# Three intermediates of a recurrent layer kept in PSUM between VectorE's steps

## The chip, the cores and the metric

The kernel runs on one core of a Trainium2 chip. The metric is device time in microseconds (us), as the median of several runs. Engines are named as in the profile: PE (TensorE, matmuls), PEld (its weight loads), DVE (VectorE), ACT (ScalarE), POOL (GpSimd), and SP, which here only issues DMAs. SBUF is the large on-chip memory; PSUM is the small one that matmuls write, used here as eight banks of 128 partitions by 512 fp32 values. PE, DVE and ACT work on PSUM here; POOL and DMAs work on SBUF only.

## The reference

Two layers of a decoder, 512 tokens, width 1024, all in fp32. Layer 0 is an RWKV-7 time mixing: token-shifted mixes of the normalised input go through four projections (r, k, v and a gate g), and then a recurrence runs over time for each of 16 heads, with a 64x64 state:

```python
def step(state, inp):
    r_t, w_t, k_t, v_t, kk_t, a_t = inp
    s_kk = jnp.einsum('bhij,bhj->bhi', state, kk_t)
    state = (state * w_t[:, :, None, :]
             - s_kk[..., None] * (kk_t * a_t)[:, :, None, :]
             + v_t[..., None] * k_t[:, :, None, :])
    return state, jnp.einsum('bhij,bhj->bhi', state, r_t)
```

Its result y is normalised per head, a bonus term is added, and it is multiplied by silu(g) and projected by `w_out`. Each layer ends with a gated per-layer embedding ("ple"). Layer 1 is a causal differential attention on keys and values projected from layer 0's result. Only layer 0 is touched here.

## The kernel before

**Dense products.** Every projection is made of 128x512 blocks. For accuracy an fp32 operand is split into a high and a low part in fp32r, and one block product is three matmuls (lines 285, 286 and 287: high by high, high by low, low by high). I call such a triple a block; 800 of them make up most of PE's work. Weights arrive by DMA (`RAW`), ACT or DVE rounds the high part (line 270) and POOL or DVE subtracts it to get the low part (line 318).

**The recurrence, in chunks.** Time is cut into 8 chunks of 64 tokens, and the 16 heads into two groups of 8 (g = 0 and 1). `gram` multiplies keys by queries inside a chunk pair (line 984) and DVE masks the result into SBUF tiles `G` (line 993). `inverse(n)` inverts the small triangular matrices, for four batches of (group, half of time): it gathers 32x32 blocks of `G` into a tile `na` (line 270, on ACT or DVE by a planner's choice), loads a unit matrix `eye32` by DMA and copies it by ACT into a PSUM bank `xs` (line 1030), transposes `na` on DVE (line 1042), does 31 steps of substitution on DVE (lines 1051 and 1054), transposes back (1060, 1075) and finishes with two rounds of 32x32 matmuls on PE (1087, 1101) and small copies back into `G` (270 and 1115, eight of these on ACT). `operands` transposes the keys of a chunk (1149, 1152). `recur(g)` then does one chunk after the other: products with `G` (1188), the product with the state `S_` (1201), two pairs of copies from PSUM (270) with a product between them, the update product `pS` (1229), and the new state on DVE: the sum with `pS` (line 1241) and the decay (line 1244). `finish(cq, g)` normalises y (1284 to 1293), transposes it on PE (1304), adds a bias and multiplies by the gate on DVE (line 1310), and splits the result `zF` into high (270) and low (1318) for the output projection.

**What sets the order.** All this is written as Python generators. A planner (`Streams`) runs while the program is built: each `yield` names an engine (or two to choose from), an estimated cost, a buffer taken or freed, or an event; the planner keeps a clock for each engine and always takes the step that can start first, by its own estimates. A `+` after an engine's name means that the step also takes a port that the planner shares between DVE and POOL. The instructions stand on each engine's queue in the order in which the planner took them, and each queue runs in order. So a change of a cost, an engine or a buffer in one place can move instructions of the whole stage. Buffers are counted: 43 slots `R` and 9 slots `H` in SBUF, and eight PSUM banks, four for dense blocks (`pd`) and four for everything else (`pw`). Dense blocks of the projections fill PE while the recurrence waits for other engines.

## Time and profile before

| | |
|---|---|
| median of 3 runs | 792.98 us (791.94 to 794.04) |
| the profiled execution | 797.09 us, span 795.3 us |
| PE busy | 756.1 us (95%) |
| DVE busy | 589.8 us (74%) |
| ACT busy | 454.5 us (57%) |
| POOL busy | 201.9 us (25%) |
| from 80 to 407 us (recurrent stage) | 327.0 us, PE busy 309.45 us, DVE 280.96 us |
| from 407 us to the end | 388.3 us, PE busy 379.04 us |

Busy time is the time in which an engine has an instruction in work. The granted clock of PE (PEclk) is 1.00 nearly everywhere and lower in a few stretches. What counts for the time is where PE has nothing to do or runs at the lower clock: all other engines have room on average, but each may be the one that PE waits for at a given place. Spans on POOL are rough.

### The profile page before, as it was taken

To read this page: it belongs to the slowest core of one execution; us is meant where nothing else is said; L and a number is where in the kernel's file an instruction comes from. 1 tells how busy PE (TensorE), PEld (TensorE's weight loads), DVE (VectorE), ACT (ScalarE), POOL (GpSimd) and SP (SyncE) were. 2 spreads that over 40 slices of the span, in tenths; PEclk is the share of its full clock that TensorE was granted. 3 is DMA by queue.
4 is the path that set the end of the run, shared out by engine and by line. 5 is a ranking of instruction groups with operands and counts; after the bars stand their busy time and mean duration, and the time that the engine had idled before them with its cause. 6 is when DMAs were issued, how large, how long until landed. Compare 5 with 4: busy or idle time off the path is not lost.

```text
span 795.3 us, 13941 instructions
## 1 busy us (share of the span) xinstructions
PE 756.1 (95%) x5016; PEld 605.1 (76%) x5016; DVE 589.8 (74%) x1360; ACT 454.5 (57%) x1078; POOL 201.9 (25%) x221
## 2 busy tenths in 40 slices
PE   6899999998999899999989999999999999999996
PEld 3576578875777677777778888887888888888884
DVE  2989999976798898998676685446874768835844
ACT  3779745688875446664444564333764566743431
POOL 2416615521451425666010010000000001100000
PEclk9999999998999899999999999999999999999998
DMA  8585669843684687463446444488943523314602
GB/s 325 197 285 196 245 225 290 298 147 105 209 286 171 217 301 258 145 228 105 133 166 247 133 146 135 172 309 226 312 158 92 159 53 121 117 43 159 259 6 106
DMA packets 66677, 148.79 MB, mean 187 GB/s; under 512 B 6576, under 2 KB 27312, under 8 KB 66608
## 3 DMA queue, kind: packets, MB, share of 16 engines
q1 hardware_dynamic: 43824, 112.25, 41.9%
q10 hardware_dynamic: 22784, 35.66, 13.1%
q8 instruction: 39, 0.64, 0.3%
q14 instruction: 30, 0.25, 0.1%
HBM read 110.13 MB, written 37.75 MB: 186 GB/s over the span
## 4 chain that ended last, share of the span: by engine, by line
PE 70%; DVE 8%; ACT 8%; DMA 8%; issue 2%; POOL 2%; SPq 1%; ACTq 0%; POOLq 0%; DVEq 0%
PE p L285 18%; PE p L287 18%; PE p L286 18%; PE p L1788 2%; PE p L984 2%; PE p L1188 2%; ACT R L270 1%; PE p L1753 1%; PE p L1752 1%; PE p L1201 1%; DMA R<-bD 1%; PE p L1779 1%; DMA RAW<-in_ple_w 1%; PE p L1410 1%; DMA R<-mD 1%
## 5 line engine op out<-in xcount | busy, mean ns | idle before, releaser
L285 PE MATMUL p<-R,R 128*128 128x512 f32 x800 | 326.4, 408 | 3.2 <-DVE R L270 1.7
L286 PE MATMUL p<-R,R 128*128 128x512 f32 x800 | 314.1, 393 | 3.8 <-DVE R L525 3.6
L287 PE MATMUL p<-R,R 128*128 128x512 f32 x800 | 314.4, 393 | 0.0
L285 PEld LDWEIGHTS p<-R,R 128*128 128x128 f32 x800 | 151.3, 189 | 37.1 <-DVE R L270 1.9
L287 PEld LDWEIGHTS p<-R,R 128*128 128x128 f32 x800 | 151.0, 189 | 33.2 <-DVE R L1318 0.4
L286 PEld LDWEIGHTS p<-R,R 128*128 128x128 f32 x800 | 151.5, 189 | 32.4 <-DVE R L525 4.9
L318 POOL TENSOR_TENSOR R<-RAW,R 128x512 fp32r<-128x512 f32 x59 | 78.6, 1339 | 163.3 <-ACT R L270 89.1
L270 ACT CAST R<-RAW 128x512 fp32r<-128x512 f32 x110 | 66.1, 619 | 26.7 <-DMA RAW<-in_w_g 10.0
L318 DVE TENSOR_TENSOR R<-RAW,R 128x512 fp32r<-128x512 f32 x81 | 56.8, 715 | 11.0 <-ACT R L270 10.2
L324 DVE SCALAR_TENSOR_TENSOR R<-RAW,vec,R 128x512 fp32r<-128x512 f32 x64 | 46.6, 748 | 13.9 <-ACT R L322 13.7
L322 ACT ACTIVATE R<-RAW,vec 128x512 fp32r<-128x512 f32 x64 | 44.6, 720 | 17.0 <-DMA RAW<-in_b_w_in 9.1
L1397 POOL TENSOR_TENSOR hr<-hm,half 128x1 f32<-128x1 f32 x16 | 10.4, 648 | 147.2 <-DVE hm L1395 147.2
L1757 DVE CUSTOM_DVE_ANT_0 p<-p,cmask 128x128 f32<-128x128 f32 (+3 forms) x64 | 30.3, 509 | 17.4 <-PE p L1753 17.3
L1764 ACT ACTIVATE H<-p,mx 128x128 f32<-128x128 f32 (+3 forms) x64 | 33.3, 526 | 15.7 <-DVE mx L1761 14.1
L281 POOL TENSOR_TENSOR orr<-orm,half 128x4 f32<-128x4 f32 x8 | 8.4, 1055 | 123.3 <-DVE orm L279 93.3
L1054 DVE TENSOR_TENSOR p<-p,H 128x126 f32<-128x126 f32 (+22 forms) x124 | 32.6, 263 | 4.3
L1051 DVE TENSOR_TENSOR H<-p,R 128x126 f32<-128x126 f32 (+22 forms) x124 | 30.5, 246 | 1.1
L1534 DVE SCALAR_TENSOR_TENSOR R<-H,R 128x512 f32<-128x512 f32 x16 | 11.1, 691 | 24.5 <-ACT H L1527 23.1
L1527 ACT ACTIVATE H<-p 128x512 f32<-128x512 f32 x16 | 9.5, 596 | 31.6 <-PE p L287 31.6
L521 DVE SCALAR_TENSOR_TENSOR p<-R,vec,p 128x511 f32<-128x511 f32 x32 | 23.5, 747 | 5.4 <-ACT p L519 5.3
L519 ACT ACTIVATE p<-R,omm 128x512 f32<-128x512 f32 x32 | 22.0, 695 | 5.0 <-DVE R L525 3.7
L1788 PEld LDWEIGHTS p<-R,H 128*128 128x128 f32 x160 | 22.1, 191 | 2.8 <-ACT H L1805 0.5
(227 smaller groups left out, 1249.4 us busy)
## 6 DMA issues: line engine op xcount, KB each, us to landing
R<-mD SPq DMA_DIRECT2D x40, 512.0 KB, 5.3
mD<-R ACTq DMA_DIRECT2D x32, 512.0 KB, 4.3
RAW<-in_ple_gate SPq DMA_DIRECT2D x16, 512.0 KB, 3.7
RAW<-in_kv_w SPq DMA_DIRECT2D x16, 512.0 KB, 3.9
RAW<-in_b_w_in SPq DMA_DIRECT2D x16, 512.0 KB, 3.9
R<-bD ACTq DMA_DIRECT2D x24, 256.0 KB, 5.2
R<-in_x SPq DMA_DIRECT2D x8, 512.0 KB, 6.8
RAW<-in_w_r SPq DMA_DIRECT2D x8, 512.0 KB, 4.0
```

What stands on the lines that cost most here:

```text
L270: (nc.scalar.copy if sc.eng == "ACT" else ENG[sc.eng].tensor_copy)(dst, src)
L285: nc.tensor.matmul(ps, ah, bh, start=first, stop=False)
L286: nc.tensor.matmul(ps, ah, bl, start=False, stop=False)
L287: nc.tensor.matmul(ps, al, bh, start=False, stop=last)
L318: ENG[sc.eng].tensor_sub(lo, f, hi.bitcast(F32))
L322: nc.scalar.activation(hi, f, AF.Copy, scale=g)
L324: nc.vector.scalar_tensor_tensor(lo, f, g, hi.bitcast(F32), ALU.mult, ALU.subtract)
L1051: ve.tensor_mul(tmp[:, 0:m, 0:w], bc(xs[:, s_ : s_ + 1, 0:w], [P, m, w]), bc(nb[:, s_ + 1 : 32, s_ : s_ + 1], [P, m, w]))
L1054: ve.tensor_add(xs[:, s_ + 1 : 32, 0:w], xs[:, s_ + 1 : 32, 0:w], tmp[:, 0:m, 0:w])
L1757: nc.vector.tensor_tensor_reduce(scs[m][:, 0:n], scs[m][:, 0:n], cmask[:, S - n : S], 1.0, -3.0e38, ALU.add, ALU.max, mx[:, m : m + 1])
L1764: nc.scalar.activation(E[m][:, 0:n], scs[m][:, 0:n], AF.Exp, bias=mx[:, m : m + 1], scale=0.125, accum_out=sm[:, m : m + 1])
L1788: nc.tensor.matmul(po[:, x * P : (x + 1) * P], aT[:, kb * P : (kb + 1) * P], vT[hg, kb // 2][:, kb % 2, x * P : (x + 1) * P], start=(kb == 0),
```

## The change

Three intermediates, all of layer 0's recurrent stage, go from SBUF tiles to PSUM banks. In `inverse`, the gathered tile `na` is a PSUM bank, taken before the gathering; the unit matrix stays in its SBUF slot until the gathering is done, and ACT's copy of it into `xs` now stands behind the gathering; `xs` takes its bank only then. One `H` slot fewer is taken. In `recur`, the sum of state and `pS` is written into `pS`'s bank instead of into the state, and the decay reads it from there. In `finish`, the gated result is written over its own PSUM input, which is held until both halves of the split have read it; the high part is always made by ACT and the low part always by DVE. The planner's marks and costs for these steps change with them (`DVE+!` to `DVE!`, the transpose's 2.0 to 1.14).

```diff
-        yield "take", "H", 3
-        na, xs, tmp = HT([P, 16, 32]), HT([P, 32, 16]), HT([P, 31, 16])
+        yield "take", "H", 2
+        eye, tmp = HT([P, 32, 16]), HT([P, 31, 16])
         yield "DMA!", 0.4
-        nc.sync.dma_start(xs, I["eye32"])
-        if eng == "DVE":
-            yield "take", "pw", 1
-            eye, xs = xs, bank("pw").rearrange("p (s c) -> p s c", c=16)
-            yield "ACT!", 0.52
-            nc.scalar.copy(xs, eye)
-            yield "free", "H", 1
+        nc.sync.dma_start(eye, I["eye32"])
+        yield "take", "pw", 1
+        na = bank("pw").rearrange("p (h t) -> p h t", t=32)
         for u in range(2):
             yield "wait", ("gram", 2 * cp + u, g)
             for hh in range(2):
                 for q, r in enumerate(quads):
-                    yield "ACT/DVE+!", (0.2, 0.2)
+                    yield "ACT/DVE!", (0.2, 0.2)
                     copy(four(na[r, 8 * u + 4 * hh : 8 * u + 4 * hh + 4]), lower(q, u, hh)[:, :, :, 32 * (q % 2) : 32 * (q % 2) + 32])

+        yield "take", "pw", 1
+        xs = bank("pw").rearrange("p (s c) -> p s c", c=16)
+        yield "ACT!", 0.52
+        nc.scalar.copy(xs, eye)
+        yield "free", "H", 1
         yield "take", "R", 1
         nb = R([P, 32, 32])
-        yield "DVE", 2.0
+        yield "DVE", 1.14
         nc.vector.transpose(nb, bc(na.rearrange("p h t -> p t h").unsqueeze(2), [P, 32, 2, 16]))
-        yield "free", "H", 1
+        yield "free", "pw", 1
...
                     if c_ > 0:
                         yield "DVE!", 0.42
-                        nc.vector.tensor_add(sv, sv, qv)
-                        qv = sv
-                    yield "DVE+!", 0.42
+                        nc.vector.tensor_add(qv, qv, sv)
+                    yield "DVE!", 0.42
                     nc.vector.tensor_mul(sv, qv, bc(pcall[hs, c_, 4 * g : 4 * g + 4].unsqueeze(2), [HN, 4, HN]))
...
         for x in range(4):
             xs = slice(x * P, (x + 1) * P)
-            nc.vector.scalar_tensor_tensor(w[:, xs], pt[:, xs], vcol(V_LB, 4 * g + x), gt[:, xs], ALU.add, ALU.mult)
-        yield "free", "pw", 1
+            nc.vector.scalar_tensor_tensor(pt[:, xs], pt[:, xs], vcol(V_LB, 4 * g + x), gt[:, xs], ALU.add, ALU.mult)
...
-        yield "ACT/DVE+", (0.52, 0.34)
-        copy(hi, w)
-        yield "Pool+/DVE+", (1.23, 0.6)
-        ENG[sc.eng].tensor_sub(lo, w, hi.bitcast(F32))
+        yield "ACT", 0.48
+        nc.scalar.copy(hi, pt)
+        yield "DVE", 0.6
+        nc.vector.tensor_sub(lo, pt, hi.bitcast(F32))
+        yield "free", "pw", 1
```

Lines behind the first hunk are moved by one: 1042, 1060, 1087, 1101, 1115, 1152, 1188, 1201, 1229 and 1241 are now 1043, 1061, 1088, 1102, 1116, 1153, 1189, 1202, 1230 and 1242; the copy of the unit matrix goes from 1030 to 1038. From line 1244 on the numbers are the same up to 1310; the split's two lines are now 1315 and 1317.

The planner's order moves with the change, from the gathering of the first inverse on to the end of layer 0's recurrence; in the rest of the program PE's blocks stand in the same order. Three places are shown. Names are a tile's pool (`p` for a PSUM bank, `R` and `H` for SBUF slots) with a number.

The first is ACT's queue at the gathering of the fourth batch; line 1501 empties the banks of the embedding's products. Before:

```order
L1501 COPY H_2970<-p_2935 128x512
L1501 COPY H_2983<-p_2969 128x512
L1030 COPY p_3010<-H_2994 128x512
L270 COPY H_2993<-R_2877 32x128 x3
L270 COPY H_2993<-R_2878 32x128 x3
L1501 COPY H_3005<-p_2982 128x512
L1501 COPY H_3042<-p_3004 128x512
```

And now:

```order
L1501 COPY H_2974<-p_2949 128x512
L270 CAST R_2995<-RAW_2669 128x512
L1501 COPY H_3012<-p_2973 128x512
L1501 COPY H_3027<-p_3011 128x512
L1501 COPY H_3056<-p_3026 128x512
L270 CAST R_3057<-RAW_2846 128x512
L270 COPY p_2979<-R_2961 32x128 x3
L270 COPY p_2979<-R_2962 32x128 x3
L1038 COPY p_3098<-H_2965 128x512
```

The copy of the unit matrix, which needs a DMA, stood ahead of the last two copies of line 1501 and of the gathering; it now stands behind all of them.

The second is ACT's queue behind the second inverse, from its last small copy (1115, now 1116) to the copy (270, out of a `p` bank into `H`) on which the recurrence's next product waits. Before:

```order
L1115 COPY R_1206<-p_1987 32x2x2x32
L1115 COPY R_1206<-p_1988 32x2x2x32
L787 ACTIVATE p_1939<-H_1862 128x512
L270 COPY H_2087<-p_1992 64x2x128
L789 ACTIVATE R_1460<-H_1862 128x4x128
```

And now:

```order
L1116 COPY R_1217<-p_1991 32x2x2x32
L1116 COPY R_1217<-p_1992 32x2x2x32
L872 COPY H_2060<-p_1491 128x512
L872 COPY H_2086<-p_1499 128x512
L523 CAST R_1997<-p_1998 128x512
L519 ACTIVATE p_2008<-R_116,omm_97 128x512
L270 COPY H_2106<-p_2089 64x2x128 x2
```

One ACT instruction stood between them, and half of the copy; now four stand there and the whole copy. Ahead of these rows, from the two copies behind line 1087's matmuls (now 1088) on, ACT's queue holds in the new order four copies of line 1153, one of 872, two of 866, one of 519, nine of 270 and the eight of 1116. On PE, between line 1088's matmuls and the product that waits, now stand four transposes, three blocks and the matmuls of 1102, 1189, 1202 and 824, and a fourth block whose bank the first copy of line 872 shown above empties.

The third is PE's queue at the end of the recurrence: the transposes of the last y (line 1304) and the first block that reads what `finish` makes of it (`R_4621` before, `R_4612` now). Before:

```order
L285 MATMUL p_4363<-R_4282,R_4554 128x512
L286 MATMUL p_4363<-R_4282,R_4554 128x512
L287 MATMUL p_4363<-R_4282,R_4554 128x512
L1304 MATMUL p_4610<-ident_89,R_4101 128x128 x4
L285 MATMUL p_4461<-R_4222,R_4621 128x512
```

And now:

```order
L1304 MATMUL p_4597<-ident_89,R_4082 128x128 x4
L285 MATMUL p_4449<-R_4298,R_4511 128x512
L286 MATMUL p_4449<-R_4298,R_4511 128x512
L287 MATMUL p_4449<-R_4298,R_4511 128x512
L285 MATMUL p_4449<-R_4306,R_4511 128x512
L286 MATMUL p_4449<-R_4306,R_4511 128x512
L287 MATMUL p_4449<-R_4306,R_4511 128x512
L285 MATMUL p_4449<-R_4363,R_4511 128x512
L286 MATMUL p_4449<-R_4363,R_4511 128x512
L287 MATMUL p_4449<-R_4363,R_4511 128x512
L285 MATMUL p_4506<-R_4272,R_4612 128x512
```

No block stood between them, and three do now; counted from the recurrence's last product (line 1188, now 1189), 11 blocks stood ahead of that reading block and 16 do now. On DVE, between the transposes of lines 1042 and 1075 of the third batch, the queue holds one instruction less of each of the lines 684, 993, 1069 and 270, all moved behind that stretch or to ACT. The last six products with the state (1201) stood 11, 11, 8, 7 and 5 blocks apart on PE, and now stand 6, 7, 8, 6 and 5 blocks apart.

More of the change, by code (lines that the diff above doesn't have):

```diff
@@ L1060, in inverse @@
         nc.vector.transpose(xr, bc(xs.unsqueeze(3), [P, 32, 16, 2]))
-        yield ("free", "pw", 1) if eng == "DVE" else ("free", "H", 1)
+        yield "free", "pw", 1
         yield "take", "H", 3
@@ L1314, in finish @@
         hi, lo = (zF[cq, g][:, n].rearrange("p a b -> p (a b)") for n in range(2))
-        yield "ACT/DVE+", (0.52, 0.34)
-        copy(hi, w)
-        yield "Pool+/DVE+", (1.23, 0.6)
-        ENG[sc.eng].tensor_sub(lo, w, hi.bitcast(F32))
+        yield "ACT", 0.48
+        nc.scalar.copy(hi, pt)
+        yield "DVE", 0.6
+        nc.vector.tensor_sub(lo, pt, hi.bitcast(F32))
+        yield "free", "pw", 1
         yield "free", "R", 1
```

## The prediction

> **What bounds the kernel now.** I read the page's busy times first, then a table by stretch, then what ended PE's idle time.
>
> ```profile
> PE 756.1 (95%) x5016; PEld 605.1 (76%) x5016; DVE 589.8 (74%) x1360; ACT 454.5 (57%) x1078; POOL 201.9 (25%) x221
> PE   6899999998999899999989999999999999999996
> PEclk9999999998999899999999999999999999999998
> ```
>
> PE is busy for 95% of the span, and the digits fall below 9 only in a few slices; in two of them PEclk falls too. PE is the bound, so only its idle time and its slow clock can be won. The next rows give, for each stretch, its length, busy time (and count) of PE, PEld, DVE, ACT, POOL, then the granted clock, the share of the DMA engines and GB/s.
>
> ```profile
> 187.10:193.80 6.70, 5.31 (x29) 3.91 (x31) 5.39 (x9) 6.44 (x17) 1.38 (x1) 0.53 0.04 7
> 265.60:272.40 6.80, 6.37 (x27) 5.28 (x28) 5.06 (x13) 5.11 (x13) 3.76 (x3) 0.53 0.46 155
> 250.50:292.85 42.35, 37.62 (x186) 30.08 (x185) 37.59 (x118) 18.12 (x38) 15.04 (x12) 0.92 0.70 249
> 480.00:520.00 40.00, 40.00 (x180) 33.09 (x179) 20.64 (x31) 14.58 (x25) 0.95 (x1) 1.00 0.51 167
> 80.00:407.00 327.00, 309.45 (x2886) 241.69 (x2886) 280.96 (x663) 202.87 (x497) 135.41 (x145) 0.98 0.62 211
> 407.00:795.30 388.30, 379.04 (x1882) 316.88 (x1881) 248.17 (x597) 193.89 (x479) 34.88 (x40) 0.99 0.47 154
> ```
>
> The change touches only the stage from 80 to 407 us. There PE idles 327.0 - 309.45 = 17.6 us, and two stretches of 6.7 and 6.8 us run at a clock of 0.53, which costs a busy PE up to 6.8 x 0.47 = 3.2 us each. So the most that any change here could win is about 24 us; DVE, though busy for 281 of 327 us, is worth only what PE waits for it. The 480 to 520 row gives the price of a block at full clock: 40 us / 180 matmuls x 3 = 0.67 us. The next rows are PE's idle times in this stage that bear on the change: start, length, instruction, and in brackets the idle time before it and what ended it.
>
> ```profile
> 185.48 0.50 PE L749 MATMUL p<-R,R 128*128 128x512 f32 x1 [1.81 <-ACT R L1115]
> 187.13 1.12 PE L1188 MATMUL p<-H,R 128*64 128x64 f32 x16 [0.48 <-DVE H L270]
> 189.61 0.79 PE L285 MATMUL p<-R,R 128*128 128x512 f32 x1 [1.35 <-DVE R L800]
> 266.03 2.08 PE L984 MATMUL p<-R,R 64*128 64x128 f32 x16 [3.12 <-ACT H L1501]
> 292.85 1.20 PE L1087 MATMUL p<-H,R 32*32 32x32 f32 x64 [1.61 <-DVE H L1075]
> 308.83 1.16 PE L1201 MATMUL p<-R,R 128*128 128x128 f32 x8 [0.76 <-DVE R L1244]
> 355.41 1.16 PE L1201 MATMUL p<-R,R 128*128 128x128 f32 x8 [0.84 <-DVE R L1244]
> 389.09 0.50 PE L285 MATMUL p<-R,R 128*128 128x512 f32 x1 [1.68 <-DVE R L270]
> ```
>
> Both slow stretches begin in or right after such a wait: behind the second inverse (1.81 + 0.48 + 1.35 = 3.64 us idle) and at the gathering of the fourth (3.12 us). These two places carry most of what can move.
>
> **The instructions themselves.** Groups of the stage: line, engine, operation, count, then busy us and mean ns of one.
>
> ```profile
> L1244 DVE TENSOR_TENSOR R<-R,pcall 64x256 f32<-64x256 f32 x24 | 15.2, 633 | 0.7
> L1244 DVE TENSOR_TENSOR R<-p,pcall 64x256 f32<-64x256 f32 x4 | 1.7, 415 | 0.5 <-PE p L1229 0.5
> L1241 DVE TENSOR_TENSOR R<-R,p 64x256 f32<-64x256 f32 x24 | 10.0, 416 | 2.0 <-PE p L1229 1.7
> L1042 DVE STREAM_TRANSPOSE R<-H 128x1024 f32<-128x1024 f32 x4 | 8.3, 2080 | 0.2
> L1060 DVE STREAM_TRANSPOSE R<-p 128x1024 f32<-128x1024 f32 x4 | 5.0, 1243 | 0.1
> L270 DVE COPY H<-R 32x128 f32<-32x128 f32 x20 | 5.8, 290 | 0.3
> L1318 DVE TENSOR_TENSOR R<-R,R 128x512 fp32r<-128x512 f32 x8 | 6.4, 796 | 0.4 <-ACT R L270 0.2
> L525 DVE TENSOR_TENSOR R<-p,R 128x512 fp32r<-128x512 f32 x14 | 9.4, 681 | 0.5 <-ACT R L523 0.3
> ```
>
> The decay from PSUM exists already in four chunks: 415 against 633 ns, so 24 x 0.218 = 5.2 us of DVE less. The sum (1241) reads the same operands and writes the bank instead; I take its price as unchanged. A transpose from PSUM is the L1060 row, though its reading pattern differs from L1042's; between no gain and that row I take the row: 4 x 0.84 = 3.3 us less. The low part of z becomes what L525 is: 8 x 0.115 = 0.9 us less. The gathering's copies into a bank have no row; between 290 ns as now and the 415 ns of a four times wider step with a bank I take 70 ns more for some 20, or 1.4 us. DVE so loses about 8 of 281 us, nearly all of it hidden behind PE's blocks; the sum below counts only places where PE waits. The gathered tile now also holds one of four `pw` banks while `gram` (984) needs two at once and the recurrence two; PE is what would wait, at 984 or 1202, and the planner's order, from which I count below, already has the banks in it.
>
> [...]
>
> **Place 1, the gathering of the fourth batch: -4.5 us.** ACT's queue there, and SP's DMA for it:
>
> ```profile
> 258.44 0.38 SPq L1025 DMA_DIRECT2D H<-in_eye x1
> 263.02 0.59 ACT L1030 COPY p<-H 128x512 f32<-128x512 f32 x1 [4.84 <-DMA H<-in_eye]
> 265.39 1.07 ACT L1501 COPY H<-p 128x512 f32<-128x512 f32 x2
> 267.14 0.69 DVE L318 TENSOR_TENSOR R<-RAW,R 128x512 fp32r<-128x512 f32 x1 [1.82 <-ACT R L270]
> ```
>
> ACT stands for 4.84 us at the copy of the unit matrix, because its DMA lands only at 263.0. Behind it in the queue are the gathering and then the two copies of line 1501, which empty the banks that PE's line 984 needs: PE's 3.12 us and the slow stretch behind it follow from a copy that nothing needs yet. In the new order it stands behind the gathering and behind the last copy of 1501, so the wait has lost what it held up. PE's time from 250.5 to the matmuls of the third inverse (292.85) then has 42.35 - 3.12 - 1.61 - 3.2 = 34.4 us of work. But the substitution on DVE ends this stretch already now (the row at 292.85), and it is next: 37.59 us busy, plus 42.35 - 37.59 - 1.82 (the DVE wait in the last row, which ACT's delay caused) = 2.9 us of small gaps, less two transposes (1.7) and, by the order, four instructions that no longer stand in that stretch (three of about 0.7, as L525, and one copy, 2.4). That is 36.4 us, and with 1.5 us of unforeseen waiting 37.9: a gain of 4.5. Bounds: 6.5 if DVE keeps pace with PE's work more closely; 1.0 if the copies of 1501 then wait for the `H` slots whose DMAs they share, or if the weight and mix loads, at 249 GB/s in this stretch, cannot come faster.
>
> **Place 2, behind the second inverse: +2.5 us.** The durations of ACT's and PE's pieces there, from the timeline, the groups and the chain:
>
> ```profile
> 175.25 1.18 ACT L1093 COPY H<-p 32x512 f32<-32x512 f32 x2
> 177.04 0.76 ACT L1152 COPY R<-p 128x128 f32<-128x128 f32 x4
> 180.21 3.35 ACT L270 COPY R<-H 32x128 f32<-32x128 f32 x11
> 183.57 2.14 ACT L1115 COPY R<-p 32x128 f32<-32x128 f32 x8
> 170.65 0.74 ACT L270 COPY H<-p 64x256 f32<-64x256 f32 x2 [1.07 <-PE p L1201]
> L872 ACT COPY H<-p 128x512 f32<-128x512 f32 x4 | 2.4, 593 | 0.0
> L519 ACT ACTIVATE p<-R,omm 128x512 f32<-128x512 f32 x14 | 9.6, 698 | 2.3 <-DVE R L525 2.2
> 154.30 1.13 PE p L1101 x64
> 169.47 1.09 PE p L1201 x8
> 96.05 0.99 PE p L824 x8
> ```
>
> Counted from the end of the inverse's first matmuls, ACT's new queue is 1.18 + 0.76 + 0.6 (872) + 3 x 0.7 (866 and 519) + 9 x 0.305 + 2.14 = 9.5 us; the next copy (872) ends at 10.1 and frees a bank for PE's fourth block; another 872, 523, 519 and the awaited copies bring it to 10.1 + 0.6 + 0.6 + 0.7 + 0.74 = 12.7. PE needs 0.6 (transposes) + 3 x 0.67 + 1.13 + 0.6 + 1.09 + 0.99 = 6.4 us to its fourth block: it waits 3.7, and after that block (10.8) another 1.9 for the product. That makes 5.6 us idle against 3.64 now, so +2.0, and 0.5 for a slow stretch that starts earlier under it. Bounds: -1.0 (ACT may have a part of the list behind it by then) and +5.2 (a second slow stretch, 3.2 us more).
>
> **Place 3, the state: 0.** The two waits for line 1244, 0.76 and 0.84 us, should shrink with a decay that is 0.2 us shorter twice per chunk, -0.8; but the new order sets the last six products with the state 6, 7, 8, 6 and 5 blocks apart, where 11, 11, 8, 7 and 5 stood, so that less work covers the same chain of copies, and I set +0.8 against it. Bounds: -1.6 and +2.5.
>
> **Place 4, the tail: -1.7 us.** The block at 389.09 waits 1.68 us for z; in the new order three more blocks, 2.0 us, stand ahead of it. The high part now always comes from ACT, whose copies of a bank take 593 ns (L872); that fits under the three blocks. Bounds: -2.2 and 0.
>
> The first inverse's stretch (PE 100% busy) and the rest behind 407 us, whose order does not move, count zero. Sum: -4.5 + 2.5 + 0 - 1.7 = -3.7 us. The profiled execution took 797.09 us, with 1.8 us around its span, and would take 793.4; it lies 4.1 us over the median of the runs, and I take the difference over to the median: 792.98 - 3.7 = 789.3 us.
>
> **The rivals.** Differences within 0.3% (2.4 us) count as no change.
> (a) Both slow stretches go. If ACT is not behind at place 2 (its list there was 10.5 us long before and PE still lost only 3.64), no slow stretch forms: -3.7 - 2.5 - 2.0 = about -8 us, 785. For it: the shorter DVE steps bring each inverse forward. Against it: 5.6 us of idle in some 12 us by the sum above.
> (b) PE's work decides. What one place wins, the next one waits for, since PE idles at only 5% and the dense blocks are loaded at their own pace; or the reordering does nothing but shuffle waits. 793, no change.
> (c) Slower. ACT's list at place 2 grows past PE's cover by more than the sum says and a second slow stretch follows it (+2.0 + 3.2 + 0.5), while the DVE substitution takes the place of ACT's wait at place 1 with only 1 us won and the tighter recurrence eats the tail's gain: +4.7 us, 797.7. It decides from the point at which PE's idle time behind the second inverse passes some 6 us. For it: ACT is continuously busy there already (3.35 and 2.14 us in a row). Against it: place 1's wait is gone by position, not by a duration.
>
> **How the numbers follow.** The forecast (787 to 790.6) gets 0.40, (a) 0.16, (b) 0.25, (c) 0.19. So faster is 0.56, same 0.25, slower 0.19. The range of 8 in 10 goes from 783.5 (beyond a) to 797.0 (most of c); the forecast's own is 786.5 to 791.5.
>
> **What would show it.** Right: no ACT wait for the unit matrix's DMA over 1 us, clock 1.00 around the fourth gathering, the third inverse's first matmuls still released by line 1076 (before 1075) and 4 to 5 us earlier against the last gather; 4 to 6 us of PE idle behind the second inverse, ended by ACT's lines 872 and 270; no idle above 0.5 us at the block that reads the last z; decay at 415 ns and the gathered transpose near 1.25 us. Wrong: a slow stretch at a new place, line 1501 still late because of `H` slots, or waits of line 1202 for 1244 that grow past 2.5 us in all.

## The result: 0.7% slower, not 0.5% faster

The changed kernel takes 801.38 us (median of 16 runs, 797.89 to 805.85) against 796.12 us for the kernel before on the same chip (16 runs, 791.94 to 801.43). The ratio is 1.0071 with a 95% interval of 1.0052 to 1.0089: slower by about 5.7 us, where 3.7 us less was forecast, and outside the forecast range. The forecast started from 792.98 us, the median of three runs, which lies 3.1 us under the median of the sixteen; a range moved up by as much would end at 800.1, still below the result. The page of the changed kernel, busy times and slices:

```profile
PE 762.2 (95%) x5016; PEld 609.2 (76%) x5016; DVE 588.3 (73%) x1362; ACT 453.2 (56%) x1083; POOL 194.5 (24%) x214
PE   6899999998889999998999999999999999999996
PEclk9999999998989998999999999999999999999999
```

DVE has become 1.5 us shorter and PE 6.1 us longer, with as many matmuls as before. The clock falls below 9 in three slices of the first half where it fell in two.

The profiles need a caution. The profiled execution of the changed kernel took 805.42 us (span 803.6) and is the second slowest of its sixteen; its granted clock is 0.984 on average, where the median of the sixteen is 0.9885. The kernel before was profiled at 0.989, while 29 of its runs, taken beside the first experiments, have a median of 0.987. So the two spans lie 8.3 us apart where the medians of the times lie 5.3 apart, and over the runs the changed kernel is not granted a lower clock than the kernel before. What the tables below say of slow stretches holds for this pair of executions.

The loss lies in the stage of layer 0. By the start of one and the same dense block (the 346th of line 285), that stage ends at 413.0 us before and 421.0 now; the end of the span is 8.3 us later. The table by stretch (length, then busy us and count of PE, PEld, DVE, ACT, POOL, granted clock, DMA share, GB/s), first of the kernel before, to that block:

```profile
80.00:413.00 333.00, 315.45 (x2918) 246.75 (x2918) 285.28 (x669) 204.94 (x501) 135.96 (x146) 0.98 0.62 209
```

And of the changed kernel: the stage, three pieces of it at half the clock, and the 42.35 us that end where the third inverse's first matmuls start, which answer to the row 250.50:292.85 of before:

```profile
80.00:421.00 341.00, 321.09 (x2922) 250.01 (x2921) 283.64 (x672) 203.52 (x506) 128.60 (x139) 0.97 0.60 204
190.40:197.20 6.80, 5.54 (x30) 2.78 (x31) 3.64 (x6) 5.51 (x14) 2.10 (x2) 0.51 0.19 77
231.30:238.10 6.80, 6.48 (x58) 5.80 (x59) 2.88 (x5) 2.35 (x6) 2.81 (x7) 0.51 0.81 261
316.40:323.20 6.80, 6.80 (x136) 5.59 (x134) 5.87 (x11) 5.73 (x16) 4.95 (x5) 0.51 0.74 254
255.00:297.35 42.35, 40.97 (x243) 32.66 (x239) 36.98 (x124) 23.79 (x60) 15.39 (x13) 1.00 0.71 247
```

The stage is 8.0 us longer. PE's idle time in it goes from 17.6 to 19.9 us, 2.4 more. PE's busy time grows by 5.6: three slow stretches cost (5.54 + 6.48 + 6.80) x 0.49 = 9.2 us where two cost (5.31 + 6.37) x 0.47 = 5.5, which is 3.7 of it; by the clocks of the runs above, nothing of these 3.7 is to be seen in the medians. Some 1.9 us of longer matmul records are not placed.

PE's waits in the stage (its timeline; start, length, instruction, and in brackets the idle time before and what ended it):

```profile
164.31 0.69 PE L1189 MATMUL p<-H,R 128*64 128x64 f32 x16 [1.23 <-ACT H L270]
191.66 1.94 PE L824 MATMUL p<-H,hsel 128*32 128x512 f32 x8 [3.98 <-ACT R L1116]
212.02 0.69 PE L1189 MATMUL p<-H,R 128*64 128x64 f32 x16 [2.27 <-ACT H L270]
231.62 1.12 PE L1189 MATMUL p<-R,R 128*64 128x64 f32 x16 [2.46 <-ACT R L1249]
297.37 1.20 PE L1088 MATMUL p<-H,R 32*32 32x32 f32 x64 [0.79 <-DVE H L1076]
315.16 1.16 PE L1202 MATMUL p<-R,R 128*128 128x128 f32 x8 [1.86 <-DVE R L1244]
362.28 1.16 PE L1202 MATMUL p<-R,R 128*128 128x128 f32 x8 [0.52 <-DVE R L1244]
367.06 0.69 PE L1189 MATMUL p<-H,R 128*64 128x64 f32 x16 [1.55 <-DVE H L270]
398.41 0.50 PE L285 MATMUL p<-R,R 128*128 128x512 f32 x1 [0.17 <-ACT R L1315]
414.80 0.66 PE L1410 MATMUL p<-ident,R 128*128 128x128 f32 x4 [0.84 <-DVE R L1469]
```

The wait of the fourth gathering (3.12 us) is gone and that of the last z is down from 1.68 to 0.17, as forecast. The waits at 164, 212 and 231 us stand where before none was longer than 0.62 us, the one at 315 us answers to one of 0.76, and the slow stretches at 231 and 316 us are new.

The instructions came near the prices that the forecast gave them. Groups of the changed kernel's stage (count, busy us, mean ns):

```profile
L1244 DVE TENSOR_TENSOR R<-p,pcall 64x256 f32<-64x256 f32 x28 | 11.8, 421 | 0.8
L1242 DVE TENSOR_TENSOR p<-p,R 64x256 f32<-64x256 f32 x24 | 10.4, 432 | 6.0 <-PE p L1230 5.5
L1043 DVE STREAM_TRANSPOSE R<-p 128x1024 f32<-128x1024 f32 x4 | 5.0, 1242 | 0.0
L1317 DVE TENSOR_TENSOR R<-p,R 128x512 fp32r<-128x512 f32 x8 | 5.5, 686 | 2.1 <-ACT R L1315 2.0
L270 ACT COPY p<-R 32x128 f32<-32x128 f32 x47 | 12.2, 260 | 20.1 <-DVE R L993 10.3 <-DVE p L270 7.6 <-DVE R L525 1.3
L270 DVE COPY p<-R 32x128 f32<-32x128 f32 x17 | 5.0, 292 | 6.5 <-ACT p L270 6.3
```

Two of the prices that the forecast started from were means of unlike things. The views of single lines give the shortest, the median and the longest instruction in ns: the decay and the gathering's copies on VectorE before, and these copies now:

```profile
L1244 DVE TENSOR_TENSOR R<-R,pcall x24: 407/422/1280, 177.6 to 372.0; 64x256 f32<-64x256 f32 x24
L270 DVE COPY H<-R x20: 204/217/1014, 101.6 to 270.7; 32x128 f32<-32x128 f32 x20
L270 DVE COPY p<-R x17: 282/289/300, 101.9 to 277.8; 32x128 f32<-32x128 f32 x17
```

Of the 24 decays that read the state in SBUF, 16 took 407 to 422 ns, as long as those that read a bank. The other eight took 854 to 1280, and these eight, and no others, began while GpSimd had a TENSOR_TENSOR of 128x512 in work. A decay that reads the bank is not shorter (421 ns in the mean); what is gone is the long ones: none of the 28 took over 428 ns, though seven of them began beside such work of GpSimd. The gathering's usual copy has become 72 ns longer (217 to 289), and two copies of 885 and 1014 ns, both begun beside such work of GpSimd, are gone.

So a part that takes less of VectorE, ScalarE and GpSimd made the whole slower. The experiments ask why.

### The profile page after: what moved, and what is told of

It is laid out like the page before. It is cut to its first block, busy times and chain, and to the rows that moved or that the text cites. A ratio compares the mean times of both kernels' runs of the same rounds, so it can differ in the third digit from the quotient of the medians.

```text
span 803.6 us, 13951 instructions
## 1 busy us (share of the span) xinstructions
PE 762.2 (95%) x5016; PEld 609.2 (76%) x5016; DVE 588.3 (73%) x1362; ACT 453.2 (56%) x1083; POOL 194.5 (24%) x214
## 4 chain that ended last, share of the span: by engine, by line
PE 52%; DVE 10%; DMA 5%; issue 2%; ACT 2%; POOL 2%; ACTq 0%; SPq 0%; DVEq 0%; POOLq 0%
PE p L285 14%; PE p L287 13%; PE p L286 13%; PE p L1788 2%; PE p L1189 2%; DVE p L1055 1%; PE p L1753 1%; DVE R L318 1%; PE p L1752 1%; DVE H L1052 1%; DMA R<-bD 1%; PE p L1202 1%; PE p L1779 1%; PE p L1410 1%; DMA RAW<-in_ple_w 1%
## 5 line engine op out<-in xcount | busy, mean ns | idle before, releaser
L318 POOL TENSOR_TENSOR R<-RAW,R 128x512 fp32r<-128x512 f32 x56 | 75.1, 1349 | 159.5 <-ACT R L270 76.5
L270 ACT CAST R<-RAW 128x512 fp32r<-128x512 f32 x107 | 63.8, 618 | 23.2 <-DMA RAW<-in_w_g 8.7
L1757 DVE CUSTOM_DVE_ANT_0 p<-p,cmask 128x128 f32<-128x128 f32 (+3 forms) x64 | 30.3, 509 | 17.6 <-PE p L1753 17.4
L1055 DVE TENSOR_TENSOR p<-p,H 128x126 f32<-128x126 f32 (+18 forms) x124 | 32.6, 263 | 4.3
L1052 DVE TENSOR_TENSOR H<-p,R 128x126 f32<-128x126 f32 (+18 forms) x124 | 30.5, 246 | 1.1
L1189 PEld LDWEIGHTS p<-R,R 128*64 128x64 f32 x512 | 18.0, 140 | 9.6 <-issue 4.7
```

The costliest lines, as they stand in the source:

```text
L270: (nc.scalar.copy if sc.eng == "ACT" else ENG[sc.eng].tensor_copy)(dst, src)
L318: ENG[sc.eng].tensor_sub(lo, f, hi.bitcast(F32))
L1052: ve.tensor_mul(tmp[:, 0:m, 0:w], bc(xs[:, s_ : s_ + 1, 0:w], [P, m, w]), bc(nb[:, s_ + 1 : 32, s_ : s_ + 1], [P, m, w]))
L1055: ve.tensor_add(xs[:, s_ + 1 : 32, 0:w], xs[:, s_ + 1 : 32, 0:w], tmp[:, 0:m, 0:w])
L1189: nc.tensor.matmul(out[HALF[par][ii % 2 ^ x], cols(ii, hh)], G[cq, hh, g][:, ii, par, o : o + HN], rhs[:, cols(ii, hh)], start=start and n ...
L1757: nc.vector.tensor_tensor_reduce(scs[m][:, 0:n], scs[m][:, 0:n], cmask[:, S - n : S], 1.0, -3.0e38, ALU.add, ALU.max, mx[:, m : m + 1])
```

## The experiments

**Theory O** says that the loss comes from the plan that the planner makes anew when any mark or cost changes: the order on each queue and, where a step may go to either of two engines, the sharing. I call both together the order. **Theory I** says that it comes from the instructions themselves and from the banks that are held longer. "Before" below is the run of the kernel before beside each experiment; ratios are to it, with 95% intervals.

### Order and instructions of the state, apart

The change edits the state in two ways: the sum goes into the bank, and the decay loses the planner's mark `+`. The first run has the sum alone (the first diff), with the marks and so the order of before; the second the mark alone (the second diff), with every step's work as it was; the third has both, in the second's order.

```
-                        nc.vector.tensor_add(sv, sv, qv)
-                        qv = sv
+                        nc.vector.tensor_add(qv, qv, sv)
```

```
-                    yield "DVE+!", 0.42
+                    yield "DVE!", 0.42
```

> The state's sum stays in PSUM, all planner marks as before, so every engine's queue holds the same instructions in the same order as before; only the sum's output and the decay's input move to the bank. Theory O (the loss is the planner's new order): 0 to -2 us against before, since the decay costs 0.2 us less 24 times and two waits of PE on it (0.76 and 0.84 us) shrink. Theory I (the instructions or the banks themselves cost): +2 us or more.

> No instruction is changed: only the planner's mark of the decay loses its plus, so the planner orders the stage anew. Theory O: the order alone moves the time by several us, either way; a loss of +2 to +6 us would look like the change. Theory I: within 1 us of before.

> The state part of the change with its marks; PE's queue is that of the run with the marks alone. Theory O: as the marks alone, less 0 to 2 us. Theory I: +2 us or more over the marks alone.

| | old order | new order |
|---|---|---|
| state's instructions of before | 1 | 1.0096 [1.0074, 1.0117], 804.29 us |
| state's instructions of the change | 0.9978 [0.9957, 1.0000], 793.34 us | 1.0033 [1.0016, 1.0049], 798.74 us |

One mark, with every step's work as it was, costs 0.96% of 796 us, 7.6 us. (The new order also shares some steps anew: VectorE has 1350 instructions in place of 1360, ScalarE 1089 in place of 1078.) The new instructions win some 1.8 us in the one order and 5.5 us (804.29 - 798.74) in the other. In PE's timeline of the second run stand new waits of the kind that the changed kernel has:

```profile
251.09 1.12 PE L1188 MATMUL p<-H,R 128*64 128x64 f32 x16 [4.87 <-ACT H L270]
348.26 1.16 PE L1201 MATMUL p<-R,R 128*128 128x128 f32 x8 [2.42 <-DVE R L1244]
```

The second shows one way in which an order costs. Ahead of the decay on VectorE stands a subtraction that took 5.22 us, where the median of its kind in the kernel before is 0.69; from before its start until 345.69 us GpSimd worked on five TENSOR_TENSORs of 128x512 in a row (VectorE's timeline of that run):

```profile
341.02 5.22 DVE L1318 TENSOR_TENSOR R<-R,R 128x512 fp32r<-128x512 f32 x1
```

Theory I falls for the state, the part with the most instructions.

### The other parts alone, and the mark put back

The fourth run is the kernel before with the inverses' part of the change, the seventh with the part of `finish`, the eighth with nothing but the unit matrix's copy behind the gathering:

```
-        if eng == "DVE":
-            yield "take", "pw", 1
-            eye, xs = xs, bank("pw").rearrange("p (s c) -> p s c", c=16)
-            yield "ACT!", 0.52
-            nc.scalar.copy(xs, eye)
-            yield "free", "H", 1
         for u in range(2):
...
+        if eng == "DVE":
+            yield "take", "pw", 1
...
+            nc.scalar.copy(xs, eye)
+            yield "free", "H", 1
         yield "take", "R", 1
```

The fifth is the changed kernel with the decay's mark as it was:

```
-                    yield "DVE!", 0.42
+                    yield "DVE+!", 0.42
```

> Only the inverse's part of the change. Theory O: no sum of parts holds; the time depends on the order that comes out, anywhere from -4 to +6 us, and the wait for the unit matrix at the fourth gathering (3.1 us of PE idle and a slow stretch) is gone in the profile. Theory I: if the inverse's banks are what costs, +4 to +6 us, with PE waiting for gram's or the recurrence's banks.

> The kernel before with one part of the change: the gated results stay in the bank (lines 1310 to 1318: the step writes the bank, the high part always by ScalarE, the low part always by VectorE out of the bank). My forecast's step: the wait of 1.68 us for the last z goes, 1.7 us less, 794.3 against 796. Theory O: the planner's order from the first finish on is a new one, so anything from 3 us less to 6 us more. Theory I for this part (a bank held 0.5 us longer per block): 0 to 1 us more, with PE's waits for a free bank growing.

> The kernel before with one part of the change: ScalarE's copy of the unit matrix (lines 1026 to 1031) is written behind the gathering, which keeps its SBUF tile. Place 1 of the forecast rests on this position alone: ScalarE's wait of 4.84 us for that DMA, PE's 3.12 us and the half-rate stretch at the fourth gathering should go, as in the changed kernel; by itself 4 to 7 us less at that place. Theory O: the order behind it is new as well, so the total may keep that (789 to 792) or give it back later (796 to 800); the offset of the dense blocks against the kernel before, block by block, shows which.

> [...] No instruction differs from the changed kernel; only the order that the planner writes does. Theory O (the loss of the change is the order that the planner makes, and the order is made anew by every mark): the time leaves the changed kernel's 801.4 us by several us, to about 793 (796 less the 2.7 us that the state's instructions won in the old order); an order nobody has seen may also come out anywhere between 791 and 801. Theory I (the instructions and the longer held banks cost the 5 us): the time stays at 801 within 1.5 us, since instructions and banks are the same.

| run | median us | ratio to before |
|---|---|---|
| inverses only | 799.60 | 1.0032 [1.0017, 1.0048] |
| finish only | 798.27 | 1.0025 [1.0004, 1.0047] |
| unit copy later | 801.65 | 1.0080 [1.0054, 1.0106] |
| changed kernel, old mark | 799.17 | 1.0045 [1.0025, 1.0064] |

Each part alone loses in the order it gets, and the three edits together (0.7%) lose no more than the unit copy's move alone (0.8%). Yet that run shows the gain of place 1 at its place. The same length of time, 42.35 us, chosen to end before its third inverse:

```profile
245.00:287.35 42.35, 42.35 (x314) 34.36 (x313) 38.52 (x124) 23.02 (x57) 16.63 (x14) 1.00 0.72 247
```

No idle time and the full clock, against 4.73 us idle and 0.92 before. It is lost again at other places of that order. In the run of the inverses alone much of the gain goes at the end of the stage (PE's timeline):

```profile
388.16 0.63 PE L1305 MATMUL p<-ident,R 128*128 128x128 f32 x4 [3.72 <-DVE R L1294]
390.47 0.80 PE L285 MATMUL p<-R,R 128*128 128x512 f32 x1 [1.68 <-DVE R L270]
```

The finish alone does not even remove the wait that it was to remove. In its order the block that reads the last z waits 2.25 us for line 1315, where the kernel before waited 1.68 (PE's timeline of that run):

```profile
393.73 0.51 PE L285 MATMUL p<-R,R 128*128 128x512 f32 x1 [2.25 <-ACT R L1315]
```

The wait of place 4 went by the blocks that the full change's order put ahead of it. With the mark put back the time came out about 2 us lower, within what the two intervals leave open, and not at 793. These runs fit theory O, but in the inverses and in `finish` the new instructions were not run in the old order, so there these runs do not rule theory I out.

### ScalarE's list behind the second inverse

The sixth and ninth runs leave out the second batch's 24 small copies, in the changed kernel and in the one before, every other instruction in its order:

```
-                    copy(lower(q, u, hh)[:, :, :, 32 * (q % 2) : 32 * (q % 2) + 32], four(xm[quads[q], sl]))
+                    n == 1 or copy(lower(q, u, hh)[:, :, :, 32 * (q % 2) : 32 * (q % 2) + 32], four(xm[quads[q], sl]))
...
-                    nc.scalar.copy(
+                    n == 1 or nc.scalar.copy(
                         lower(2 * j, u, hh)[:, :, :, 32:64],
```

The tenth moves 8 of them from ScalarE to VectorE in the changed kernel; the eleventh does so in the first run's kernel:

```
-                    nc.scalar.copy(
+                    (nc.vector.tensor_copy if n == 1 else nc.scalar.copy)(
```

> The changed kernel, in which the second batch's inverse leaves out its small copies: the 16 of line 270 back into the matrix's halves and the 8 of line 1116, some 5 us of ScalarE's list and 1 us of VectorE's; the second batch's results so are not the reference's. Every other instruction stands in the same order. If ScalarE's list is what PE waits for behind the second inverse: PE's idle time of 3.98 us there and the half-rate stretch that goes with it are gone, and also the 1.23 and 2.27 us behind them if these are the same debt: 4 to 9 us less than the changed kernel, 792 to 797. If PE's own dependences make the waits (its fourth block needs something else that is late), the idle time stays within 1 us and so does the time, 801.

> The control to the changed kernel without the second batch's copies, which took 794.1 us, 7.3 less than the changed kernel: the same 24 small copies (16 of line 270, 8 of line 1115) of the second batch left out of the kernel before, every other instruction in its order; the second batch's results so are not the reference's. My forecast's place 2 says that the change made the waits there dearer by 2.5 us (bounds -1.0 to 5.2), so the same omission should win 7.3 - 2.5 = 4.8 us here: 791.2 against 796. If the second inverse cost before just what it costs now, it wins 7 us (789) and the loss of the change lies elsewhere. If the whole loss of the change comes from there (5.7 us and place 1's gain on top), it wins next to nothing (794 to 796), though 3.64 us of PE's idle time and a half-rate stretch stand there.

> The changed kernel with 8 instructions moved to another engine and nothing else: the copies of line 1116, in the second batch alone, are issued on VectorE, which stands idle for 2.61 us there, instead of ScalarE, whose list they make 2.1 us longer. The results are the reference's and PE's order is the same. If ScalarE's list is what PE waits for: the idle time of 3.98 us at the matmuls of line 824 falls by about 2, and with luck the half-rate stretch behind it goes: 2 to 5 us less than 801.4. If the copies out of the banks are merely awaited by whoever needs them, the idle time stays, since VectorE gets to them no sooner: 800 to 802.

> A candidate to beat both: the kernel before, with the state's sum left in its bank in the old order (the run of 793.3 us), and in the second batch the 8 copies of line 1115 on VectorE instead of ScalarE. If ScalarE's list behind the second inverse costs PE its 3.64 us of waits and the half-rate stretch, 2 to 4 us less than 793.3: 789 to 791. If VectorE's own list there (line 270's waits on it) becomes what ends last, 793 to 795.

| run | median us | ratio to before |
|---|---|---|
| changed, copies left out | 794.14 | 0.9983 [0.9959, 1.0007] |
| before, copies left out | 790.55 | 0.9945 [0.9922, 0.9969] |
| changed, 8 copies on VectorE | 798.73 | 1.0035 [1.0012, 1.0058] |
| first run's kernel, 8 copies on VectorE | 794.07 | 0.9977 [0.9950, 1.0005] |

Leaving the copies out wins 0.88% in the changed kernel (1.0071 to 0.9983), 7.0 us, and 0.55%, 4.4 us, in the kernel before. The difference, 2.6 us, is what place 2 was forecast to cost more, 2.5; but its interval, some 3 us to each side when the three intervals are combined, holds zero too. Moving 8 of the copies wins 1.0071 - 1.0035 = 0.36%, 2.9 us (with an interval of some 2.3 us to each side). PE's timeline of that run:

```profile
190.81 1.94 PE L824 MATMUL p<-H,hsel 128*32 128x512 f32 x8 [2.91 <-ACT H L872]
210.33 0.69 PE L1189 MATMUL p<-H,R 128*64 128x64 f32 x16 [2.28 <-ACT H L270]
228.09 0.69 PE L1189 MATMUL p<-R,R 128*64 128x64 f32 x16 [0.23 <-ACT R L1249]
```

The wait behind the inverse falls from 3.98 to 2.91, half of what was expected. The one at 231 us, 40 us later, falls from 2.46 to 0.23. It is tempting to call it the same debt. What stands behind it, in the timelines of GpSimd, of SyncE's queue and of ScalarE, first in the changed kernel:

```profile
221.30 1.28 POOL L318 TENSOR_TENSOR R<-RAW,R 128x512 fp32r<-128x512 f32 x1 [3.08 <-ACT R L270]
222.60 4.51 SPq L301 DMA_DIRECT2D RAW<-in_ple_w  x2
229.82 0.62 ACT L270 CAST R<-RAW 128x512 fp32r<-128x512 f32 x1 [3.44 <-DMA RAW<-in_ple_w]
```

And with the 8 copies moved:

```profile
220.92 4.50 SPq L301 DMA_DIRECT2D RAW<-in_ple_w  x2
226.29 0.62 ACT L270 CAST R<-RAW 128x512 fp32r<-128x512 f32 x1 [1.60 <-DMA RAW<-in_ple_w]
```

GpSimd waits 3.08 us for ScalarE's half of a weight split and reads the chunk until 222.58; only then is its `RAW` slot free, and the next load is issued at 222.60. ScalarE then stands for 3.44 us at the head of its own queue for that load, and behind it waits the copy of line 1249 that PE needs. With the copies moved the load is issued 1.7 us earlier, but by then everything stands 1.7 us earlier: counted from PE's product behind the wait of 2.28 us, the issue comes 10.58 us later in the changed kernel (222.60 - 212.02), 10.59 with the copies moved (220.92 - 210.33) and 10.59 with the copies left out (216.27 - 205.68). What differs is the load itself. ScalarE's cast starts 7.2 us behind the issue in the changed kernel, 5.4 us with the copies moved and 5.7 us without them. So PE's wait at 231 us follows the time that one load took in the profiled execution; why it took longer there is not shown, and neither is that ScalarE's list had a part in it. In the run without the copies the wait is 0.57 us and the slow stretch there is gone: from 220 to 240 us its clock is 1.00, where the changed kernel's is 0.83 (table by stretch of the run without them):

```profile
220.00:240.00 20.00, 19.35 (x256) 15.11 (x255) 14.24 (x31) 8.80 (x29) 6.06 (x11) 1.00 0.72 241
```

The wait of 2.27 us at 212 us stays in both runs (2.28), so it does not come from this list. In the order of before, where ScalarE's list was met by 3.64 us of waits too, the same move won nothing: line 1115, on VectorE, ended a wait of 1.91 us of PE, where on ScalarE, in the first run, it ended one of 1.79.

### The planner's costs

> The changed kernel with the planner's costs of the inverse's small copies set to what the trace shows: 0.30 us on ScalarE and 0.22 on VectorE for line 270's into the halves, 0.27 and 0.22 for the gathering, 0.27 for line 1116, in place of 0.2 everywhere. No instruction's work is changed; the planner may give copies to the other engine and writes a new order. If the stalls of the changed order come from the planner's belief that ScalarE is sooner done than it is (12.7 us of list counted as some 10), the order made with the true costs loses less: 793 to 797, with PE's idle time behind the second inverse under 3 us. If any new order is a draw, the time comes out anywhere between 793 and 806 and the waits stand somewhere else.

```
-                    yield "ACT/DVE+!", (0.2, 0.2)
+                    yield "ACT/DVE+!", (0.3, 0.22)
```

and likewise for the gathering and line 1116. The changed kernel's time then is 795.54 us, 1.0000 [0.9980, 1.0019]: the whole loss is gone with the order. But the wait behind the second inverse is not under 3 us (PE's timeline of that run):

```profile
189.68 1.11 PE L1150 MATMUL p<-ident,R 128*128 128x128 f32 x4 [4.17 <-ACT R L1116]
```

So the true costs did not mend what they were meant to mend; another order came out, and it was a better one. It holds the change's instructions and its longer held banks and is level with the kernel before, so these do not by themselves cost the 5.7 us.

### Is the old order a lucky draw?

The last six runs change one cost in the planner's table by 0.02 us and no step's work; the planner writes a new order, some of its sharing with it. Each such change is made to the kernel before and to the changed kernel. They are the copies of y (a), the state's sum (b), and the products of the recurrence (c), in this order:

```
-                yield "ACT!", 0.3
+                yield "ACT!", 0.32
...
-                        yield "DVE!", 0.42
+                        yield "DVE!", 0.44
...
-            yield "PE!", 0.55
+            yield "PE!", 0.57
```

> The kernel before, with one cost in the planner's table changed by 0.02 us (the copies of y behind the recurrence, 0.30 to 0.32). Nothing that any engine does is changed, only the order. If the old order was a lucky draw among the planner's orders: 798 to 804 here too, against 795.5 to 796. If orders are worth about the same and the change's own moves lose: 795 to 797.

> The changed kernel with the same 0.02 us in the planner's table. If the order is a draw: anywhere between 793 and 804, not bound to 801.4; and if the change's instructions are worth the 2.7 to 5.5 us that two pairs of one order showed, below its sister with the instructions of before on the average of the three pairs. If the change's own moves lose: 800 to 803 again.

> As the first, by another cost: the state's sum (line 1240) 0.42 to 0.44. Lucky draw: 798 to 804. Orders alike: 795 to 797.

> The changed kernel with that cost, line 1241, 0.42 to 0.44. The order a draw: 793 to 804; the change's own moves lose: 800 to 803.

> As the first null order, by a third cost: the products of the recurrence on TensorE 0.55 to 0.57. Lucky draw: 798 to 804. Orders alike: 795 to 797.

> The changed kernel with that cost, 0.55 to 0.57. The order a draw: 793 to 804; the change's own moves lose: 800 to 803.

| cost changed | kernel before | changed kernel |
|---|---|---|
| none | 1 | 1.0071 [1.0052, 1.0089] |
| a | 1.0094 [1.0066, 1.0122], 805.19 us | 1.0165 [1.0146, 1.0184], 810.06 us |
| b | 1.0110 [1.0087, 1.0132], 805.90 us | 1.0017 [1.0000, 1.0034], 797.97 us |
| c | 1.0155 [1.0116, 1.0194], 807.69 us | 1.0028 [1.0007, 1.0048], 797.72 us |

With 0.02 us in a table, the kernel before becomes 7.5 to 12 us slower, three times out of three, and with the mark alone a fourth time (1.0096). Its own order is better than all of these; whether by luck, or because it was once picked among many, is not on record. The changed kernel's orders reach from 1.0017 to 1.0165 here, and the one that it got lies among them. The means of the three are 1.0120 and 1.0070: the change is 4 us ahead where both kernels draw a new order. With pairs at +5.7, -7.4 and -10.1 us, each of two different orders, that is no proof of a gain; but that the changed kernel is the slower whatever orders are drawn is ruled out, since in two of the three pairs it is the faster.

The stage in the table by stretch, each to the same block, of the kernel before with a, b and c, one row of each:

```profile
80.00:422.30 342.30, 321.74 (x2915) 252.41 (x2913) 282.42 (x666) 206.19 (x505) 130.86 (x140) 0.96 0.60 202
```

```profile
80.00:423.00 343.00, 320.74 (x2918) 251.28 (x2916) 284.92 (x666) 205.42 (x503) 136.55 (x147) 0.96 0.60 203
```

```profile
80.00:424.70 344.70, 322.31 (x2919) 250.74 (x2917) 281.68 (x673) 203.44 (x499) 131.21 (x144) 0.96 0.60 202
```

And of the changed kernel with a, with b and with c:

```profile
80.00:423.90 343.90, 316.36 (x2916) 248.13 (x2915) 291.87 (x669) 203.09 (x502) 129.77 (x142) 0.98 0.59 202
```

```profile
80.00:413.10 333.10, 313.81 (x2918) 245.38 (x2916) 280.09 (x670) 201.85 (x504) 129.27 (x142) 0.99 0.62 209
```

```profile
80.00:410.50 330.50, 314.35 (x2918) 244.65 (x2916) 276.64 (x655) 204.97 (x512) 141.88 (x149) 0.99 0.63 211
```

The slow orders of before have 3 to 5 us more idle time than its own (20.6 to 22.4 against 17.6) and 5 to 7 us more of busy PE, at a clock of 0.96 in place of 0.98. Their other executions were granted little too: the medians over all of a kernel's runs are 0.9835, 0.982 and 0.9795 with a, b and c, and 0.986 to 0.987 for the kernel before beside them. The changed kernel with a has 27.5 us of idle time at 0.98. The changed kernel with c has 16.2 us of idle time and a clock of 0.99; its profiled execution is 2.9 us shorter in span than that of before (792.4 against 795.3), though the median of its runs is not below. In these runs an order's price was its waits and, in some orders, a slow clock beside them (0.96 against 0.98).

No kernel that left nothing out was clearly below both; the sum in the bank in the old order (0.9978 [0.9957, 1.0000]) comes nearest.

## Why the prediction was wrong, step by step

The step that failed is the sum's frame: that it suffices to count the places where the change's waits stood before, and that the remaining waits of the stage count zero. Between 160 and 250 us, outside the second inverse's own wait, PE idled 6.8 us (1.23, 2.27, 2.46, and 0.47 and 0.39 at 218 and 222) where it had idled 1.4, and a slow stretch came on top (6.48 x 0.49 = 3.2 us): +8.6 us that no term held. In its place the runs showed that the order as a whole sets the time: one mark, or 0.02 us in the planner's table, moves the kernel before by 7.5 to 12 us, and the changed kernel's instructions took from 795.54 to 810.06 us, by the order alone.

The rest, by the ledger of waits and slow stretches. It is a ledger of the two profiled executions, and its slow stretches are of this pair; which of its waits make the 5.7 us of the medians stays open.

- **Place 1, -4.5 forecast, -6.3 measured.** Right, near its lower bound of -6.5. From 4.73 us idle to 1.38 in the 42.35 us, and no slow stretch (3.0). The sum had left 37.9 - 34.4 = 3.5 us of waiting for VectorE's substitution; that came smaller. The eighth run, in an order of its own, shows the same gain from the position of one copy.
- **Place 2, +2.5 forecast, +0.5 at the place.** The first wait was worked out at 3.7 and came as 3.98, though ended by line 1116 rather than 872. The second (1.9) did not come there, and the wait of 2.46 us 40 us later is not it: that one follows a load that took 7.2 us. The price of the list's debt over all (2.6 us more than before, by the runs without the copies) fits the term, within an interval too wide to prove it.
- **Place 3, 0 forecast, +4.1 measured, beyond its bound of +2.5.** The waits of 1202 for 1244 grew from 1.60 to 2.38 us in all, inside what I called right; but the one of 1.86 us was followed by a slow stretch of 6.80 x 0.49 = 3.3 us. The tighter spacing, which I set at +0.8, has no part in it: this product is not among the last six, and 63 blocks stand between it and the one before it, where 64 did. VectorE's queue is what I had not followed. First the changed kernel, then the one before (VectorE's timelines):

```profile
312.66 1.69 DVE L1072 SCALAR_TENSOR_TENSOR H<-R,rowm,H 128x512 f32<-128x512 f32 x1
314.26 0.84 DVE L1244 TENSOR_TENSOR R<-p,pcall 64x256 f32<-64x256 f32 x2
```

```profile
307.95 0.83 DVE L1244 TENSOR_TENSOR R<-p,pcall 64x256 f32<-64x256 f32 x2
308.81 1.16 DVE L1071 SCALAR_TENSOR_TENSOR H<-R,rowm,H 128x512 f32<-128x512 f32 x1
```

A step of the third inverse stood behind the two decays that PE waits for; now it stands ahead of them, and takes 1.69 us in place of 1.16 (the step before it, line 1070, takes 1.45 in place of 0.82; GpSimd had a TENSOR_TENSOR in work beside both). The -0.8 for shorter decays had no ground here either: these two took 0.83 us together before and 0.84 now. Other waits of that part, at 367 to 378 us, added 1.5 us.
- **Place 4, -1.7 forecast, -1.5 measured.** Right in the changed kernel's order, by the three blocks. Line 1410, which I did not count, won 1.35 more.
- **The instructions.** The prices now are right: decay 421 ns (415 forecast), transpose 1242 (1243), low part 686 (681), sum 432 (416). Two prices before were misread. The 633 ns of a decay are the mean of 16 at 0.42 us and eight that met GpSimd, so its 5.2 us lie in eight instructions and not in 24; of the low part's mean of 796, one instruction of eight with 1533 ns makes nearly all the difference to 692. And the gathering's copies on VectorE, priced at 70 ns more, did take 72 more at the median (217 to 289 ns); their means, 292 against 290 ns, hide it, because two long copies are in the old one. ScalarE's were shorter into the bank, 260 ns, than before into SBUF, 295.
- **Behind 407 us, zero.** Right: the lead of the old kernel changes from 8.0 to 8.3 us.

These add up to 0.5 + 8.6 - 6.3 + (0.8 + 3.3 + 1.5) - 2.9 = +5.5 of the stage's 8.0 us; the rest is in small gaps and in longer records that I could not place.

Of the rivals, (c) had the sign and the price nearest, but not the mechanism: place 1 and the tail kept their gains, and the second slow stretch that it asked for as the price of ScalarE's list stands behind a late load. That its price came close is luck. What none of the cases held is that the order before was itself a good one among the planner's. Each of the four edits that touch nothing but a mark or a cost of the kernel before lost 7.5 to 12 us, so an edit should have been expected to lose something of this order before its own worth counts, and slower should have been the likeliest case.

## What to carry to other kernels

Where a planner or a scheduler writes the order, an edit is two changes: what the instructions cost, and a new draw of the order. Price the draw first, by edits that alter nothing but the order, and compare the edit within one order (keep the marks and costs of the old kernel, as the first run did) or over several. A sum over the places of the old profile cannot see the waits of the new order. Before a wait is put down to a cause, compare it in a run where the cause is taken away, counted from a common instruction: the wait at 231 us went with the copies, but not because of them. And before a mean is used as a price, look at the shortest, the median and the longest.

## What the runs showed of the hardware

**In these traces the half clock followed the idle time within one step of a raster of 3.41 us, and not the length of a wait alone.** The traces also keep each change of the granted clock. In all 20 of them, from 80 to 780 us, it changes only on a raster of 3.41 us, and the stretches at half the clock are one to four steps long. The raster lies differently against the kernel's start in each execution: below, steps begin at 207.28 us in the one and at 207.80 in the other. The tables by stretch, on the raster's steps, first of the changed kernel, then of the run with the 8 copies moved, which has the same order on PE and the same wait (2.27 and 2.28 us):

```profile
207.28:210.69 3.41, 2.47 (x29) 1.93 (x28) 2.25 (x5) 3.41 (x9) 0.84 (x2) 1.00 0.00 0
210.69:214.10 3.41, 2.08 (x22) 1.62 (x22) 2.99 (x6) 3.37 (x11) 0.03 (x1) 1.00 0.90 345
```

```profile
207.80:211.21 3.41, 1.13 (x20) 0.85 (x19) 2.91 (x5) 3.40 (x11) 0.00 (x0) 1.00 0.59 241
211.21:214.62 3.41, 3.41 (x26) 2.37 (x26) 2.95 (x5) 2.10 (x5) 2.24 (x2) 0.50 0.58 222
```

In the first the wait is split over two steps, 0.94 and 1.33 us of idle time, and the clock stays. In the second it lies whole in one, 2.28 us, and the next step runs at half the clock; so it is in the run with the copies left out, at 206.40 us. The wait of 1.86 us at 315 us lay whole in the step from 313.09 to 316.50. Of the 2267 steps at the full clock that were counted in the 20 traces, the clock fell after all 42 with 1.79 us or more of idle PE, after 9 of the 47 with 1.28 to 1.78 us, and after none of the 2178 with less. In those of the kernel before and of the changed one, from 80 to 780 us, it fell after all five with 1.80 us or more and after none of the other 393. So the length of one wait alone did not decide here (2.27 us without a drop, 2.28 with one), and the executions of one kernel differ: the sixteen of the changed kernel were granted 0.982 to 0.994.

**Beside GpSimd's TENSOR_TENSORs a step of VectorE took up to 7.6 times its median here (5.22 against 0.69 us).** The decay with two operands in SBUF took 0.41 to 0.42 us, and 0.85 to 1.28 us in the eight cases that began beside a TENSOR_TENSOR of 128x512 on GpSimd; the one subtraction of 5.22 us stood beside five of them. With one operand in a bank none of the 28 decays of the changed kernel took over 0.43 us, though seven began beside such work. Which steps met differed with the order.
